# A two-layer hybrid decoder trunk: another emission plan for the small work and the weight splits, and attention scores in two row tiles

## The chip, the cores and the metric

The kernel runs on one core of a Trainium2 chip. The metric is the time of one execution in microseconds (us), as the median of several runs on the device.

## The reference, cut to what matters

The input is 256 tokens of 1024 float32 values, the depth is 2. One layer does:

```python
h = rms_norm(x, attn_norm)
(mq, mk, mv, nq, nkv, ngate, gq, gk, gv, g_lr, g_out, merge) = split(h @ w_in)
o_moba = moba_attention(rms_norm(mq), rms_norm(mk), mv, rel_bias)       # 4 heads of 64
kc, vc = compress_tokens(k_c, ...), compress_tokens(v_c, ...)           # gelu(h @ w1) @ w2
o_nsa  = nsa_attention(rms_norm(nq), kc, vc, k_s, v_s, k_w, v_w, ...)    # 4 heads, 3 branches
o_gla  = gla_attention(gq, gk, gv, log_a)                               # 4 heads, chunks of 64
z = g_a * (o_moba @ w_moba) + g_b * (o_nsa @ w_nsa) + g_c * (o_gla @ w_gla)
x = x + z @ w_out
a, g = split(rms_norm(x) @ w_up)                                        # 2 x 2816 columns
x = x + (gelu(causal_conv3(a)) * g) @ w_down
```

With 256 tokens, MoBA's own block, the selected blocks of NSA and its window all come down to causal softmax attention over the same 256 keys, with a bias by distance. So each layer has 12 softmax heads in three branches: "s" (selected) and "w" (window) of NSA, which share the queries, and "m" (MoBA).

## The kernel before, in words

**Dense products.** Every weight goes through the core once, in blocks of 128x1024 float32 (512 KB). A block is loaded into a `raw` buffer by a DMA of SyncE. ScalarE rounds it to a high part `whi` (type fp32r), and VectorE and GpSimd write what is left, `wlo` = `raw` - `whi`, each for a share of the columns. TensorE then makes three fp32r matmuls per tile into a PSUM buffer `pd`: high by high, low weight by high activation, high weight by low activation. The activations are split in the same way into `hh` and `hl` (in the FFN's down projection `fh` and `fl`). Chunks of mode A have weights as the moving operand (512, 396, 272 or 256 columns); those of mode B have activations (256 columns): the queries and keys of GLA, and all of the FFN's up projection.

**Stages.** Per layer: the input projection (14 chunks), the three branch projections, the output projection, the up projection (22 chunks in pairs j = 0 to 10: `done_a` and `done_g`, lines 1400 and 1434), the down projection. In the up projection each pair has 96 matmuls on TensorE, and beside them VectorE does four `SCALAR_TENSOR_TENSOR` of the convolution, two products with PSUM, one cast (`fh`) and its share of four blocks' low parts; GpSimd does one product (`tt<-tt,rsB`), `fl` and the rest of the low parts.

**What sets the order.** All engines work through their instructions in the order in which the program issues them. This order is made while the program is built: `Plan` (line 51) keeps a clock for each engine (`V` VectorE, `A` ScalarE, `G` GpSimd, `PE` TensorE), `cost` (line 73) estimates an instruction, `note` (line 106) books it and when its output is there. The small work (norms, attention, GLA, evictions) is written as generators, which lie in the lists `urgent` and `normal`. `run_phase` (line 357) issues the dense matmuls and calls `tick` (line 307) after each tile, which lets those generators go on whose time has come by the plan; `avail` and `hold` (lines 200 and 205) make one wait for a planned time, `take` and `give` for a free buffer. A wait in the plan costs nothing on the chip; a wait on the chip arises where an instruction stands in an engine's order ahead of its inputs.

**Weight blocks.** `Pump` (line 218) has 5 `raw` buffers and 3 pairs of `whi`, `wlo`. When `run_phase` gets a block, loads are issued for 5 blocks from there and splits for 2. `split` (line 262) issues the high part on ScalarE and directly behind it the low part, the columns divided so that VectorE and GpSimd end together by their costs, as though neither slowed the other:

```python
v, g = max(plan.t["V"], t0) + 0.07, max(plan.t["G"], t0) + 0.1 + 0.0
m = int((v - g + c * 0.00104) / (0.00104 + 0.0023)) // 64 * 64
```

**Scores.** `softmax_branch` (line 1002) starts two generators with two heads each. `one_head` (line 1053) computes scores with a contraction over all 128 partitions: two heads' queries lie in one tile (64 partitions each), and the key tiles `kt` and `mkt` hold each head with zeros in the other half (`nsa_keys` line 879, `pair_T` with `halves` line 943; the zeros come from memsets on GpSimd at the start). Per head there is one float32 matmul with 128 columns and one with 256; the trace shows each float32 matmul as two records. Then follow the bias and row maximum (VectorE), the exponential (ScalarE), three transposes (TensorE), a copy `pT` (ScalarE) and three matmuls into `po`.

**Compression.** `compress` (line 725) multiplies 16 slices of `w1` with the tokens `xt`, which four additions on VectorE write, in two groups of eight matmuls (`pst<-tt,w`).

Line 135 (line 163 in the changed file) is the helper through which every instruction is recorded, so rows are told apart by their tiles.

Of the kernel before, what the change touches and what calls it, by code (L numbers as in the profile page):

```python
# [18 lines left out]
S = 256  # L19
# [30 lines left out]

class Plan:
# [20 lines left out]

    def cost(self, e, f, outs, ins, kw):
        n = max(_free(a) for a in outs[:1] + ins[:1]) if outs else 0
        if e == "PE":
# [3 lines left out]
            if ins[0].dtype == F32R:  # L79
                return max(0.107, m / 2400 + 0.0025)  # L80
            return max(_free(ins[0]) / 600, m / 600 + 0.004)
        if e == "V":
            if f == "reciprocal":
                return 0.07 + n * 0.0084
            if f == "tensor_tensor_scan":
                return 0.07 + n * 0.00104
# [4 lines left out]
            return 0.07 + 0.06 * ptr + n * (0.00052 if fast else 0.00104)  # L91
        if e == "S":
            return 0.06
        if e == "A":
            if f == "dma_start":
                return 0.06
            return 0.11 + n * 0.00083 + 0.05 * ("pst" in str(ins[0].tensor) or "pd" in str(ins[0].tensor)) + 0.09 * (len(outs) - 1 + hasattr(kw.get("bias"), "tensor"))
# [8 lines left out]
    def note(self, e, f, args, kw):  # L106
        outs, ins = _aps(args, kw)
        if not outs:
            return
        self.n += 1  # L110
        st = max([self.t[e], self.t["PE"]] + [self.get(a) + 0.15 for a in ins])
# [4 lines left out]
        else:  # L116
            en = st + self.cost(e, f, outs, ins, kw)
            self.t[e] = en
        lat = 0.2 if e == "PE" else 0.0
# [33 lines left out]
def trunk_kernel(ctx, tc, x, rel_bias, attn_norm, w_in, moba_q_norm, moba_k_norm,  # L153
# [61 lines left out]
    RAWB, HLB = 5, 3  # L215
    AHEAD_D, AHEAD_S = 5, 2

    class Pump:
        def __init__(self):
# [3 lines left out]
            self.auto = False  # L223

# [37 lines left out]
        def split(self):  # L262
            n, hi, lo = self.open()
            hi(0, n)
            w = self.blocks[self.ns - 1][1]
            h = self.hl[self.ns - 1][0]
            t0 = plan.get(h)
            v, g = max(plan.t["V"], t0) + 0.07, max(plan.t["G"], t0) + 0.1 + 0.0
            c = n * w
            m = int((v - g + c * 0.00104) / (0.00104 + 0.0023)) // 64 * 64  # L270
            m = c if m > c - 128 else m if m >= 128 else 0
# [11 lines left out]
        def get(self):  # L283
            i = self.ng
            self.ng += 1
            self.ahead(AHEAD_D, AHEAD_S if self.auto else 0)
            return self.hl.pop(i)
# [19 lines left out]
    def tick(n=4):  # L307
        now = plan.t["PE"]
        for g in list(urgent):
# [13 lines left out]
    def idle(limit=None):  # L323
# [3 lines left out]
        if a == (len(flags), plan.n) and plan.t["PE"] <= now:  # L327
            r = [ready.get(id(g), 0.0) for g in urgent + normal]
            r = [v for v in r if v > now] + ([limit] if limit else [])
# [285 lines left out]
    def norm_rs(st):  # L615
# [4 lines left out]
        yield  # L620
        V.tensor_scalar(st["rsh"], st["rs"], 0.5, None, op0=OP.mult)
# [19 lines left out]
    def make_layer(l):  # L641
# [41 lines left out]
        def gla_gate():  # L683
# [33 lines left out]
            setf("ln")  # L717
            V.tensor_sub(m, m, u)
# [945 lines left out]
```

## Time and profile before

| what | value |
|---|---|
| median of 3 runs | 852.81 us (852.76 to 854.57) |
| the profiled execution's own time | 854.52 us |
| its span, first to last instruction | 852.7 us |
| TensorE busy | 836.4 us (98%) |
| VectorE / ScalarE / GpSimd busy | 575.4 / 431.7 / 469.4 us |
| granted TensorE clock, mean | 0.995 of full speed |
| DMA, mean over the span | 168 GB/s, 143.57 MB |

The time outside the span is 1.8 us. A busy share is an average over all stages; matmuls overlap in the records, so a busy TensorE is not one at its peak: the number of matmuls that start in a stretch says more than the busy time.

### The profile page before, as it was taken

Reading aid. Unit: us, or ns where it says so; the run is one execution under the profiler, and the core shown is the slowest. Engines: PE = TensorE matmul, PEld = TensorE weight load, DVE = VectorE, ACT = ScalarE, POOL = GpSimd, SP = SyncE. Lnnn points to the kernel's source line nnn. Section 1 sums busy time; section 2 is a strip of 40 time slices with the busy share of each in tenths; the row PEclk is TensorE's granted clock in tenths of the full one; section 3 lists DMA queues with packets and bytes.
Section 4 is the critical chain, followed back from the end, with each engine's and each line's share of the span. In section 5 each row is a group of like instructions: output and inputs, shape, how many; then the busy total and the mean of one; then the engine's idle time right before and its main releaser. Section 6 shows DMA issues by size and latency. Waiting matters only on the chain.

```text
span 852.7 us, 13950 instructions
## 1 busy us (share of the span) xinstructions
PE 836.4 (98%) x5173; PEld 747.5 (88%) x5173; DVE 575.4 (67%) x882; ACT 431.7 (51%) x667; POOL 469.4 (55%) x338
## 2 busy tenths in 40 slices
PE   8999999999999899999999999999999999999998
PEld 7779888888899899998898898888888999999886
DVE  5676887458657878875447667764595599887632
ACT  6545555554456445443557445564544654554431
POOL 5534644546555665666545346535565476665653
PEclk9999999999999999999999999999999999999999
DMA  7893444445555465556458444545556555646561
GB/s 230 255 262 110 124 123 143 118 163 193 178 154 170 149 194 177 174 183 210 158 173 238 136 122 125 148 124 156 166 177 194 162 160 173 196 157 212 184 220 46
DMA packets 109976, 143.57 MB, mean 168 GB/s; under 512 B 13677, under 2 KB 71380, under 8 KB 109780
## 3 DMA queue, kind: packets, MB, share of 16 engines
q1 hardware_dynamic: 109892, 142.68, 53.9%
q8 instruction: 41, 0.67, 0.3%
q14 instruction: 27, 0.22, 0.1%
q10 hardware_dynamic: 16, 0.00, 0.0%
HBM read 141.60 MB, written 2.63 MB: 169 GB/s over the span
## 4 chain that ended last, share of the span: by engine, by line
PE 82%; DVE 7%; issue 1%; POOL 1%; ACT 0%; DVEq 0%; ACTq 0%; POOLq 0%
PE pd L135 72%; PE pst L135 9%; DVE tt L135 4%; DVE wlo L135 3%; PE po L135 2%; POOL tt L135 1%; ACT whi L135 0%; DVE qz L135 0%; POOL fl L135 0%; POOL wlo L135 0%; DVE fh L135 0%; DVE xs L135 0%; DVE grp L135 0%; DVE hl L135 0%; DVEq L135 0%
## 5 line engine op out<-in xcount | busy, mean ns | idle before, releaser
L135 POOL TENSOR_TENSOR wlo<-raw,whi 128x256 fp32r<-128x256 f32 (+10 forms) x219 | 315.1, 1442 | 281.0 <-ACT whi L135 268.6
L135 ACT CAST whi<-raw 128x1024 fp32r<-128x1024 f32 (+3 forms) x268 | 271.7, 1017 | 267.3 <-PE pd L135 156.7
L135 DVE TENSOR_TENSOR wlo<-raw,whi 128x768 fp32r<-128x768 f32 (+8 forms) x262 | 267.2, 1028 | 177.1 <-ACT whi L135 176.3
L135 PE MATMUL pd<-hh,wlo 128*128 128x256 f32 x768 | 218.5, 285 | 4.6 <-DVE wlo L135 4.6
L135 PE MATMUL pd<-hh,whi 128*128 128x256 f32 x768 | 219.8, 286 | 0.2
L135 PE MATMUL pd<-hl,whi 128*128 128x256 f32 x768 | 218.2, 284 | 1.1 <-DVE hl L135 1.1
L135 PE MATMUL pd<-whi,hh 128*128 128x512 f32 (+3 forms) x512 | 204.8, 400 | 1.5 <-ACT whi L135 0.7
L135 PE MATMUL pd<-wlo,hh 128*128 128x512 f32 (+3 forms) x512 | 192.7, 376 | 1.6 <-DVE wlo L135 1.2
L135 PE MATMUL pd<-whi,hl 128*128 128x512 f32 (+3 forms) x512 | 192.2, 375 | 0.0
L135 PEld LDWEIGHTS pd<-hh,wlo 128*128 128x128 f32 x768 | 148.0, 193 | 5.8 <-DVE wlo L135 5.8
L135 PEld LDWEIGHTS pd<-hl,whi 128*128 128x128 f32 x768 | 148.0, 193 | 1.8 <-DVE hl L135 1.5
L135 PEld LDWEIGHTS pd<-hh,whi 128*128 128x128 f32 x768 | 148.0, 193 | 1.3 <-ACT hh L135 0.7
L135 PEld LDWEIGHTS pd<-whi,hh 128*128 128x128 f32 x512 | 96.6, 189 | 17.3 <-ACT whi L135 1.9
L135 PEld LDWEIGHTS pd<-wlo,hh 128*128 128x128 f32 x512 | 96.8, 189 | 16.9 <-DVE wlo L135 2.6
L135 PEld LDWEIGHTS pd<-whi,hl 128*128 128x128 f32 x512 | 96.4, 188 | 17.3
L135 DVE SCALAR_TENSOR_TENSOR tt<-tt,pt 128x255 f32<-128x255 f32 x88 | 84.8, 986 | 1.6
L135 PE MATMUL pd<-whi,fh 128*128 128x512 f32 x176 | 68.7, 391 | 0.0
L135 PE MATMUL pd<-wlo,fh 128*128 128x512 f32 x176 | 68.7, 390 | 0.0
L135 PE MATMUL pd<-whi,fl 128*128 128x512 f32 x176 | 68.5, 389 | 0.0
L135 POOL TENSOR_TENSOR fl<-tt,fh 128x512 fp32r<-128x512 f32 x22 | 40.5, 1840 | 31.6 <-DVE fh L135 31.6
L135 ACT ACTIVATE tt<-tt,nm 128x128 f32<-128x128 f32 (+1 forms) x48 | 21.4, 447 | 41.0 <-DVE nm L135 41.0
L135 ACT ACTIVATE tt<-tt 128x512 f32<-128x512 f32 (+1 forms) x52 | 26.1, 532 | 31.7 <-DVE tt L135 31.6
(211 smaller groups left out, 838.7 us busy)
## 6 DMA issues: line engine op xcount, KB each, us to landing
raw<-in_w_up_dram SPq DMA_DIRECT2D x88, 512.0 KB
raw<-in_w_in_dram SPq DMA_DIRECT2D x84, 512.0 KB
raw<-in_w_down_dram SPq DMA_DIRECT2D x44, 512.0 KB
raw<-in_w_out_dram SPq DMA_DIRECT2D x16, 512.0 KB
raw<-in_w_branch_gla_dram SPq DMA_DIRECT2D x8, 512.0 KB
raw<-in_w_in_dram SPq DMA_DIRECT2D x8, 396.0 KB
raw<-in_w_branch_moba_dram SPq DMA_DIRECT2D x4, 512.0 KB
raw<-in_w_branch_nsa_dram SPq DMA_DIRECT2D x4, 512.0 KB
```

The source lines that it names most:

```text
L135: return g(*args, **kw)
```

## The change

Four things. (1) **The plan's costs** are others: TensorE's matmuls are dearer (a 512-column fp32r tile 0.227 instead of 0.216 us), outputs of VectorE and ScalarE have a delay of their own, inputs count 0.04 us behind their planned end instead of 0.15. The plan also knows intervals (`port`) in which VectorE or GpSimd read two operands from SBUF, and lengthens an instruction of the one by what it overlaps with the other's (`end`). (2) **Low parts** are not issued directly behind the high part but put into a list, from which `poll` takes them when the plan expects the high part within 0.3 us; the shares are found by trying all divisions in steps of 64 with the new lengthening and a charge on GpSimd's columns. There are 4 pairs of `whi`, `wlo`, and splits are issued 3 blocks from the one that is used. (3) **Scores** are computed for two heads together: `kt` and `mkt` hold both heads without zeros, and each matmul contracts over 64 partitions, 0 to 63 for the one head and 64 to 127 for the other, in two PSUM buffers. (4) **Compression** goes in four groups of four matmuls, and some generators wait with `avail` until an input is there by the plan.

```diff
 class Plan:
+        self.port = {"V": [], "G": []}
+        self.kind = (False, 128)
...
+    def ports(self, e, ins):
+        return e in "VG" and sum(_free(a) > 8 for a in ins) > 1 and not any(_psum(a) for a in ins)
+    def end(self, e, st, c):
+        en = st + c
+        for _ in range(4):
+            en = st + c + sum(max(0.0, min(en, b) - max(st, a)) for a, b in self.port["G" if e == "V" else "V"])
+        return en
...
             if ins[0].dtype == F32R:
-                return max(0.107, m / 2400 + 0.0025)
-            return max(_free(ins[0]) / 600, m / 600 + 0.004)
+                return max(0.112, m / 2400 + 0.0135)
+            c = max(0.112 if _free(ins[0]) < 65 else 0.224, m / 600 + 0.008)
+            return c * (0.55 if ins[0].shape[0] == 64 and m > 64 else 1.0)
...
-        st = max([self.t[e], self.t["PE"]] + [self.get(a) + 0.15 for a in ins])
+        st = max([self.t[e], self.t["PE"]] + [self.get(a) + 0.04 for a in ins])
...
+            if e == "PE":
+                k = (ins[0].dtype == F32R, ins[0].shape[0])
+                c += 0.03 * (k[0] != self.kind[0]) + 0.2 * ((k[1] == 64) != (self.kind[1] == 64))
+                self.kind = k
+            en = st + c
+            if self.ports(e, ins):
+                en = self.end(e, st, c)
+                self.port[e] = self.port[e][-30:] + [(st, en)]
             self.t[e] = en
-        lat = 0.2 if e == "PE" else 0.0
+        lat = {"PE": 0.17, "V": 0.09, "A": 0.1}.get(e, 0.03)
...
-    RAWB, HLB = 5, 3
-    AHEAD_D, AHEAD_S = 5, 2
+    RAWB, HLB = 5, 4
+    LEAD = 0.3
+    GX, PORT = 0.0005, 0.0008
+    AHEAD_D, AHEAD_S = 5, 3
...
         def split(self):
             n, hi, lo = self.open()
             hi(0, n)
-            w = self.blocks[self.ns - 1][1]
-            h = self.hl[self.ns - 1][0]
...
+            i = self.ns - 1
+            self.pend.append((i, self.hl[i][0], n, self.blocks[i][1], lo))
+        def poll(self, i=-1):
+            while self.pend and (self.pend[0][0] <= i or plan.get(self.pend[0][1]) <= plan.t["PE"] + LEAD):
+                self.low(*self.pend.pop(0)[1:])
+        def low(self, h, n, w, lo):
             c = n * w
+            best = None
+            for m in [0] + list(range(192, c + 1, 64)):
+                en = []
+                if m < c:
+                    v = max(plan.t["V"], plan.t["PE"], plan.get(h))
+                    en.append(plan.end("V", v, 0.08 + (c - m) * 0.00105))
+                if m:
+                    g = max(plan.t["G"], plan.t["PE"], plan.get(h))
+                    en.append(plan.end("G", g, 0.1 + m * 0.0023 + (GX * (c - m) if m < c else 0.0)))
+                k = max(en) + PORT * m
+                if best is None or k < best[0]:
+                    best = (k, m)
+            m = best[1]
...
     def tick(n=4):
         now = plan.t["PE"]
+        pump.poll()
...
             setf("ln")
+            yield from avail(u)
             V.tensor_sub(m, m, u)
...
-                if a == 0:
-                    yield
+                    if i % 4 == 3 and a + i < 8:
+                        yield from hold(2.0)
...
-            kt = T["kt"] = Z["kt"]
+            kt = atl("kt", [128, 2, S])
             for b in range(2):
-                for hh in range(2):
-                    r = slice(64 * hh, 64 * hh + 64)
-                    V.tensor_scalar(kt[r, b, hh], p[r, b], par[l][0][r, 20 + b:21 + b], None, op0=OP.mult)
+                V.tensor_scalar(kt[:, b], p[:, b], par[l][0][:, 20 + b:21 + b], None, op0=OP.mult)
...
+            for c in range(2):
+                yield from take(sem_t, 2)
+                yield from take(sem_ps, 2)
+                sp = pair_scores(br, c)
+                for i in range(2):
+                    normal.append(rest(2 * c + i, *sp[i]))
+                while left[0] > 2 - 2 * c:
+                    yield
...
+        def pair_scores(br, c):
...
+            sp = [(tt(), pst()) for _ in range(2)]
+            for t in range(2):
+                for i in range(2):
+                    r = slice(64 * i, 64 * i + 64)
+                    o = sp[i][1][:, 0:128] if t == 0 else sp[i][1][:, 128:384]
+                    PE.matmul(o, qT[r, t * 128:t * 128 + 128], kT[r, 0:t * 128 + 128], start=True, stop=True)
+            return sp
```

The rest of a head (`head_rest`) does what `one_head` did behind its scores. The places at which the order counts most:

VectorE at the start of the first layer's up projection, before; `tt<-tt,pt` are the convolution's four instructions of one pair j (two rows of 255 and two of 254 columns), `tt<-pd,rsB`, `tt<-tt,pd` and `fh` the other work of a pair:

```order
L135 TENSOR_TENSOR tt<-pd,rsB 128x512 x2
L135 TENSOR_TENSOR wlo<-raw,whi 128x768 x2
L135 SCALAR_TENSOR_TENSOR tt<-tt,pt 128x255
L135 SCALAR_TENSOR_TENSOR tt<-tt,pt 128x254
L135 SCALAR_TENSOR_TENSOR tt<-tt,pt 128x255
L135 SCALAR_TENSOR_TENSOR tt<-tt,pt 128x254
L135 SCALAR_TENSOR_TENSOR tt<-tt,pt 128x255
L135 SCALAR_TENSOR_TENSOR tt<-tt,pt 128x254
L135 SCALAR_TENSOR_TENSOR tt<-tt,pt 128x255
L135 SCALAR_TENSOR_TENSOR tt<-tt,pt 128x254
L135 TENSOR_TENSOR wlo<-raw,whi 128x768
L135 TENSOR_TENSOR tt<-tt,pd 128x512
```

and now:

```order
L163 TENSOR_TENSOR tt<-pd,rsB 128x512
L163 TENSOR_TENSOR wlo<-raw,whi 128x640
L163 TENSOR_TENSOR wlo<-raw,whi 128x832
L163 SCALAR_TENSOR_TENSOR tt<-tt,pt 128x255
L163 SCALAR_TENSOR_TENSOR tt<-tt,pt 128x254
L163 SCALAR_TENSOR_TENSOR tt<-tt,pt 128x255
L163 SCALAR_TENSOR_TENSOR tt<-tt,pt 128x254
L163 TENSOR_TENSOR tt<-pd,rsB 128x512
L163 TENSOR_TENSOR wlo<-raw,whi 128x640
L163 TENSOR_TENSOR wlo<-raw,whi 128x832
L163 TENSOR_TENSOR tt<-tt,pd 128x512
```

Before, the convolutions of two pairs stand in a row; now each pair's four have low parts on both sides, and the low parts on VectorE are larger.

VectorE in the first layer's input projection, before; `tt<-tt` and `b` belong to GLA's gate and wait for ScalarE's logarithm, `tt<-pst,pt 64x256` are the additions ahead of the compression, `kt` the keys:

```order
L135 TENSOR_TENSOR kn<-a_421,kss 128x2x64 x4
L135 TENSOR_TENSOR wlo<-raw,whi 128x512
L135 TENSOR_SCALAR tt<-pst,pt 128x256 x2
L135 TENSOR_TENSOR tt<-tt 128x512
L135 SCALAR_TENSOR_TENSOR b<-smask,tt 128x512
L135 TENSOR_TENSOR tt<-pst,pt 64x256 x4
L135 TENSOR_TENSOR wlo<-raw,whi 128x384
L135 TENSOR_SCALAR kt<-pst,pt 64x256 x4
```

and now:

```order
L163 TENSOR_TENSOR kn<-a_428,kss 128x2x64 x4
L163 TENSOR_TENSOR wlo<-raw,whi 128x1024
L163 TENSOR_SCALAR tt<-pst,pt 128x256 x2
L163 TENSOR_TENSOR tt<-pst,pt 64x256 x4
L163 TENSOR_TENSOR tt<-pd,nqs 128x256 x2
L163 TENSOR_TENSOR wlo<-raw,whi 128x768
L163 TENSOR_SCALAR kt<-pst,pt 128x256 x2
L163 SCALAR_TENSOR_TENSOR grp<-pd,rsB 128x512
L163 TENSOR_TENSOR tt<-tt 128x512
L163 SCALAR_TENSOR_TENSOR b<-smask,tt 128x512
```

The additions and the keys now stand ahead of the two instructions that wait for the logarithm, and the keys need two instructions instead of four.

TensorE at the first scores of branch "s" in the first layer, before (the last rows of it; the next head's scores follow three dense matmuls and a compression group later):

```order
L135 MATMUL pst<-tt,w_481 128x30 x8
L135 MATMUL pd<-whi,hh 128x512
L135 MATMUL pd<-wlo,hh 128x512
L135 MATMUL pd<-whi,hl 128x512
L135 MATMUL pst<-kt,grp 128x128
L135 MATMUL pst<-kt,grp 128x256
```

and now:

```order
L163 MATMUL pst<-tt,w_445 128x30 x4
L163 MATMUL pst<-kt,grp 128x128 x2
L163 MATMUL pst<-kt,grp 128x256 x2
L163 MATMUL pd<-whi,hh 128x512
L163 MATMUL pd<-wlo,hh 128x512
```

Two heads' scores stand together, and a compression group has four matmuls. Over the whole program VectorE's low parts grow from 262 instructions with 193032 columns to 266 with 213664, and GpSimd's go from 219 with 71608 columns to 221 with 50976; the number and sizes of the dense matmuls are the same.

## Rows read from the trace of the kernel before

**Rows 1.** The page's busy times: engine, busy us (share of the span), instructions.
```profile
PE 836.4 (98%) x5173; PEld 747.5 (88%) x5173; DVE 575.4 (67%) x882; ACT 431.7 (51%) x667; POOL 469.4 (55%) x338
```

**Rows 2.** Busy time by stretch: us, engines' busy us (instructions), granted clock, DMA share, GB/s.
```profile
25.00:60.00 35.00, 32.89 (x176) 26.02 (x175) 24.91 (x53) 17.57 (x28) 16.60 (x15) 0.99 0.89 266
60.00:120.00 60.00, 59.17 (x366) 51.93 (x366) 44.48 (x92) 31.72 (x69) 30.39 (x21) 0.98 0.41 122
...
238.00:245.00 7.00, 6.31 (x46) 5.64 (x45) 3.74 (x7) 4.79 (x10) 2.06 (x2) 1.00 0.61 188
...
262.00:298.00 36.00, 32.87 (x268) 32.07 (x268) 30.32 (x37) 17.16 (x21) 22.81 (x15) 1.00 0.49 149
...
456.00:464.00 8.00, 7.35 (x33) 5.77 (x32) 5.84 (x6) 5.15 (x7) 4.53 (x3) 1.00 0.60 177
...
650.00:690.00 40.00, 39.30 (x300) 37.62 (x299) 26.20 (x37) 23.58 (x37) 22.11 (x15) 1.00 0.56 171
690.00:740.00 50.00, 48.51 (x400) 47.90 (x399) 44.12 (x49) 24.61 (x32) 31.92 (x22) 1.00 0.56 177
...
840.00:853.00 13.00, 8.97 (x40) 7.11 (x38) 2.55 (x4) 1.05 (x1) 2.33 (x2) 0.93 0.11 42
```

**Rows 3.** The chain that ended last, pieces: start us, us, engine and tile.
```profile
179.42 28.61 PE pd L135 x126
...
245.10 8.62 PE pd L135 x72
...
297.00 0.82 DVE wlo L135
```

**Rows 4.** Timeline of DVE and POOL, first GpSimd alone, then both together.
```profile
22.45 0.73 POOL L135 TENSOR_TENSOR wlo<-raw,whi 128x256 fp32r<-128x256 f32 x1 [0.43 <-ACT whi L135]
...
262.95 0.96 DVE L135 TENSOR_TENSOR wlo<-raw,whi 128x768 fp32r<-128x768 f32 x1 [1.96 <-ACT whi L135]
262.99 1.51 POOL L135 TENSOR_TENSOR wlo<-raw,whi 128x256 fp32r<-128x256 f32 x1 [1.40 <-ACT whi L135]
...
263.82 6.72 DVE L135 SCALAR_TENSOR_TENSOR tt<-tt,pt 128x255 f32<-128x255 f32 x8
...
285.94 0.48 DVE L135 TENSOR_TENSOR wlo<-raw,whi 128x320 fp32r<-128x320 f32 x1
```

**Rows 5.** Timeline of PE in the first layer's input projection.
```profile
26.92 0.44 PE L135 MATMUL pst<-ident,ga 128*16 128x128 f32 x2 [0.62 <-ACT ga L135]
...
55.47 0.39 PE L135 MATMUL pd<-whi,hl 128*128 128x512 f32 x1
56.61 1.95 PE L135 MATMUL pst<-tt,w 128*128 128x30 f32 x16 [0.75 <-ACT whi L135]
```

**Rows 6.** Timeline of DVE in the same place.
```profile
53.80 0.69 DVE L135 TENSOR_TENSOR tt<-tt 128x512 f32<-128x512 f32 x1 [2.12 <-ACT tt L135]
...
55.67 1.72 DVE L135 TENSOR_TENSOR tt<-pst,pt 64x256 f32<-64x256 f32 x4
```

**Rows 7.** Timeline of PE: one head's scores between dense matmuls.
```profile
512.59 0.39 PE L135 MATMUL pd<-whi,hl 128*128 128x512 f32 x1
512.81 0.82 PE L135 MATMUL pst<-kt,grp 128*128 128x128 f32 x4
513.28 0.58 PE L135 MATMUL pd<-whi,hh 128*128 128x512 f32 x1
513.70 0.39 PE L135 MATMUL pd<-wlo,hh 128*128 128x512 f32 x1
```

**Rows 8.** Timeline of PE: dense ones round GLA's two gate matmuls (16 rows, 256 columns).
```profile
452.37 0.40 PE L135 MATMUL pd<-whi,hl 128*128 128x512 f32 x1
...
454.08 0.40 PE L135 MATMUL pd<-wlo,hh 128*128 128x512 f32 x1
```

**Rows 9.** Timeline of PE: compression's second product, lower and upper 64 rows.
```profile
482.85 0.39 PE L135 MATMUL pst<-w,gk 64*15 64x128 f32 x2
483.17 0.43 PE L135 MATMUL pst<-w,gv 64*128 64x64 f32 x2
```

More of the change, by code (lines that the diff above doesn't have):

```diff
@@ L48, in _span, with _psum @@
     return lo, lo + 1 + sum(abs(s) * (n - 1) for s, n in ap.ap[1:])
+def _psum(ap):
+    return any(n in str(ap.tensor) for n in ("pst", "pd_", "po_"))
 class Plan:
@@ L85, in cost @@
             if f == "tensor_tensor_scan":
-                return 0.07 + n * 0.00104
+                return 0.09 + n * 0.0021
             if f == "memset":
@@ L107, in note @@
         outs, ins = _aps(args, kw)
+        if f == "preload_act_table_set":
+            self.t[e] = max(self.t[e], self.t["PE"]) + 1.3
         if not outs:
@@ L328, in idle @@
             r = [ready.get(id(g), 0.0) for g in urgent + normal]
+            if pump.pend:
+                r.append(plan.get(pump.pend[0][1]) - LEAD)
             r = [v for v in r if v > now] + ([limit] if limit else [])
@@ L620, in norm_rs @@
         yield
+        yield from avail(st["rs"])
         V.tensor_scalar(st["rsh"], st["rs"], 0.5, None, op0=OP.mult)
@@ L742, in compress @@
             yield
+            yield from avail(kd)
             yield from take(sem_ps)
@@ L896, in nsa_keys @@
             yield from wait(("par", l))
+            yield from avail(sq)
             kn = at.tile([128, 2, 2, 2, 64], F32, name="kn", tag="kdn")
@@ L903, in nsa_keys @@
             yield
+            yield from avail(kn)
             yield from take(sem_ps)
@@ L1010, in softmax_branch, with rest @@
             sums = atl("sm" + br, [128, 2, 2, 4])
-            pend = [1, 1]
-            def heads(i):
-                for h in (i, i + 2):
-                    yield from one_head(br, h, o, sums)
-                pend[i] = 0
-            normal.append(heads(0))
-            yield
-            normal.append(heads(1))
-            while any(pend):
-                yield
+            left = [4]
+            def rest(h, s, p):
+                yield from head_rest(br, h, s, p, o, sums)
+                left[0] -= 1
+            yield from avail(*((T["mqt"], T["mkt"]) if br == "m" else (T["nq"], T["kt"])))
+            for c in range(2):
[6 more added lines that the diff above has]
+                    yield
             sh = [128, 2, 4, 64]
@@ L1059, in one_head @@
                 b = 0 if br == "s" else 1
-                qT, kT = T["nq"][:, h // 2], T["kt"][:, b, h % 2]
                 vv = lambda t: T["vs"][:, t, b]
                 bh = 4 + h
-            yield from avail(qT, kT)
-            yield from take(sem_t)
-            yield from take(sem_ps)
-            s, p = tt(), pst()
-            PE.matmul(p[:, 0:128], qT[:, 0:128], kT[:, 0:128], start=True, stop=True)
-            PE.matmul(p[:, 128:384], qT[:, 128:256], kT, start=True, stop=True)
-            yield
+            yield from avail(p)
             nm = at.tile([128, 2], F32, name="nm", tag="nm", bufs=4)
@@ L1090, in one_head @@
             yield
+            yield from avail(pT)
             PE.matmul(o[:, 0, h], pT[:, 0:128], vv(0), start=True, stop=True)
```

33 lines of the change are left out of this document (14 added, 19 removed).

## The prediction

> **What bounds the kernel now.** I read the busy times first. TensorE is busy for 836.4 of 852.7 us [rows 1], no other engine for more than 67% of the span. So the time is TensorE's own work plus the 16.3 us in which it stands still, and a change pays only if it takes work from TensorE or closes such a gap. VectorE, ScalarE and GpSimd matter only as the ones who are waited for.
>
> Second, the busy times by stretch, to see where the gaps lie. Idle is the width of a stretch less TensorE's busy time: 2.11 us in 25 to 60, 0.83 in 60 to 120, 0.69 in 238 to 245, 3.13 in 262 to 298, 0.65 in 456 to 464, 0.70 in 650 to 690 and 1.49 in 690 to 740 [rows 2]: together 9.6. The other 6.7 us of the 16.3 lie nearly all in the first 25 us and behind 840 us, and nothing in the change touches what is waited for there.
>
> Third, rates, because idle time tells less than is lost: a wait also breaks the overlap of matmuls. In an undisturbed stretch 126 dense matmuls of 512 columns take 28.61 us, 0.227 each, and 72 of 256 columns 8.62 us, 0.120 each [rows 3]. Where the compression starts, the next start comes after 1.14 us instead of 0.227: lost are 0.91 us, of which 0.75 show as idle [rows 5]. In 262 to 298, the start of the first layer's up projection, 268 matmuls ran where 36 / 0.1197 = 301 had room, so 33 x 0.1197 = 3.9 us are lost; in 690 to 740, the same place of the second layer, 50 - 400 x 0.1197 = 2.1 us [rows 2].
>
> Fourth, why there. The chain of waits runs through VectorE's low parts in that stretch, up to the last at 297.00 us [rows 3]. VectorE is busy for 30.3 of 36 us and GpSimd for 22.8 [rows 2], and the timeline shows that they are busy with waiting for each other: 256 columns of a low part take GpSimd 0.73 us alone, but 1.51 us when VectorE began its 768 columns 0.04 us earlier (0.96 us of VectorE, then the remaining 0.55); eight convolution instructions of 255 or 254 columns take 6.72 us, 0.84 each, where a low part of 320 columns takes 0.48 [rows 4]. The Trainium skill (SBUF — State Buffer, section Who interferes with whom) says the same of VectorE with two SBUF inputs against a reading GpSimd, and adds that the loser stands still until the other has finished; the 1.51 us agrees. By that rule a divided low part gains nothing from the division, and the change still divides most of them.
>
> **The change, part by part.**
>
> *Up projection (A).* In the steady part a pair j has four low parts; VectorE's share goes from 1024, 256, 768 and 768 columns to 768, 832, 832 and 1024, so 640 columns move to it from GpSimd. VectorE pays (0.96 - 0.48) / 448 = 1.07 ns per column, 0.69 us; GpSimd is spared 640 x 0.73 / 256 = 1.8 us [rows 4]. Since they exclude each other, the pair of them needs 1.1 us less per 96 matmuls, which take 11.5 us. At the start the backlog also changes: the eight convolutions in a row become twice four with low parts between, low parts no longer hold VectorE while ScalarE's high part is under way (it idled 1.96 us for one at 262.95, GpSimd 1.40 [rows 4]), and splits stand a block further ahead, which is 24 matmuls or 2.9 us. The gap to close is 3.9 + 2.1 = 6.0 us in the two layers; ends are 0 and 6.0. I take 70%, 4.2 us, because the backlog of two pairs at the start remains and only its length shrinks.
>
> *Input projection (B).* The largest gap has a cause that the new order removes: the four additions ahead of the compression ran at 55.67 us, behind two instructions of the gate for which VectorE had stood 2.12 us [rows 6]; they are now ahead of those. The transposes of `ga` (0.62 us idle [rows 5]) come three dense matmuls later. The loads of `w1` pass one weight block in SyncE's queue and are needed in four steps, so they are no new wait; DMA engines are busy 89% there [rows 2], but the bytes are the same. Between 0 and the 2.94 us of both stretches I take 2.0.
>
> *Layer seams (C).* 238 to 245, 456 to 464 and 650 to 690 lose 2.04 us. At the first and third the residual, its norm and the low part of it follow each other, which stays; the second waits for a high part, and one more block of lead covers it. I take 0.6; ends 0 and 2.04.
>
> *Scores in two row tiles (D).* A head's scores cost TensorE from the start at 512.59 to that at 513.70, less two dense matmuls: 1.11 - 0.454 = 0.66 us for 384 columns, or 1.31 for two heads [rows 7]. What it costs to switch to matmuls over fewer rows and back is seen at the gate: 1.71 - 0.454 = 1.26 us for 512 columns, which at full height would take 0.66 x 512 / 384 = 0.88, so 0.38 more [rows 8]. There are 12 pairs of heads. Without overlap a pair costs 1.31 + 0.38, in all 12 x 0.38 = 4.6 us more. With full overlap it costs 0.66 + 0.38 = 1.04, in all 3.3 us less. The nearest row on overlap shows none: the second product of the compression uses rows 0 to 63 and then 64 to 127, and the second pair of records starts 0.32 us behind the first [rows 9]; but their outputs differ in width, so another switch may lie between. Each float32 matmul is two records (x4 for two matmuls [rows 7]), and if records keep their order, the second of one head can run beside the first of the other, which makes 5 steps of 8: in units of 0.11 us for 128 columns and 0.22 for 256, 2 x 0.11 + 3 x 0.22 = 0.88 us. With the switch that is 1.26, and 12 x 0.05 = 0.6 us are gained. I take this middle value, and 4.6 more and 3.3 less as bounds. The Trainium skill (TensorEngine Tiling (Array Packing), section Key Properties) has the rule against this change: another tiling mode drains the engine. The 0.38 us agrees.
>
> *New waits (E).* The plan's allowance for inputs falls from 0.15 to 0.04 us, so some small matmuls will stand where their inputs are just late; `avail` works against it. The other engines' delays that the plan now has partly replace it. Below it is 0, above the 3.9 us of the worst stretch now; since most gaps of before are under 0.9 us and a few will open, I take 1.0.
>
> *Nothing* for the rest: two memsets on GpSimd at the start, three instructions fewer for the keys per layer and the larger `whi`, `wlo` lie beside TensorE, and the low parts that are now issued later have three blocks of lead as cover; if that lead were lost, each block would cost what rows 5 show for one wait, 0.9 us.
>
> Sum: - 4.2 - 2.0 - 0.6 - 0.6 + 1.0 = - 6.4 us. Against the profiled execution's own time of 854.5 that makes 848.1. The median of the runs is 1.7 us below that execution, so I forecast 852.8 - 6.4 = **846.4 us**.
>
> **Rivals.**
>
> *Full overlap of the tiles.* For it speaks that the two heads write to different PSUM buffers and need different rows; against it rows 9. 3.3 instead of 0.6 are gained: 843.7 us. The Trainium skill (TensorE: Matmul & The Clock Gate, Part 3) has the rule for this, that matmuls in different row groups start about 4 ns apart; no run here shows it yet.
>
> *No overlap.* The 0.32 us of rows 9 would be typical. 4.6 lost instead of 0.6 gained: 851.6 us.
>
> *The order returns nothing.* The gaps of A to C shift by a few us and remain; for it speaks that the plan is still a plan, against it that the additions of rows 6 visibly leave a wait. 852.8 - 0.6 + 1.0 = 853.2 us, no change.
>
> *Slower: VectorE becomes the bound in the up projection.* In 262 to 298 it was busy for 30.3 us in 268 / 96 = 2.8 pairs, 10.9 us per pair [rows 2]. With 0.69 us more it stands at 11.6, above the 11.5 of TensorE, if its waits for GpSimd stay as long as they are. From there every 0.1 us costs 22 x 0.1 = 2.2 us; at 11.9 us per pair 8.8 are lost and A is not returned: 852.8 - 2.2 + 8.8 = 859.4 us. It decides from 11.7 on. Against it: GpSimd reads 1.8 us less per pair, which shortens VectorE's waits.
>
> **How the numbers follow.** Forecast 0.55, its own range 842.5 to 849.5, from the ends of A to C, not all at once; full overlap 0.18; no overlap 0.11; nothing returned 0.08; VectorE the bound 0.08. The range of 8 in 10 reaches over full overlap with a good return and over no overlap, up to nothing returned: **841.0 to 853.4 us**. A measurement of this kernel can tell about 0.2%, 1.7 us, from no change. Faster by more are the first two and a part of the third: 0.77; the same 0.14; slower 0.09.
>
> **What would show it.** Right: in the first 36 us of the first up projection 290 or more matmuls start; the convolutions take clearly less than 0.84 us; no wait ahead of the compression; a pair of heads costs 1.2 to 1.3 us between dense matmuls. Wrong: VectorE's low parts still end the waits in the up projection, or a pair costs 1.7 us, or TensorE's small matmuls show new waits of more than 2 us together. The forecast falls if the seams or the first 25 us grow, which I hold as they are.

## The result, and the profile after

Four runs of the changed kernel have a median of **843.85 us** (842.90 to 844.73), four of the kernel before on the same chip 852.78; the ratio is 0.9893, 95% interval 0.9872 to 0.9914. The forecast was 846.4: the sign is right and the time lies in the forecast's own range (842.5 to 849.5), but two terms were too small and three too favourable, so that their errors in part cancelled.

The page's busy times, to be read beside [rows 1]:

```profile
PE 831.8 (99%) x5173; PEld 741.0 (88%) x5173; DVE 571.0 (68%) x880; ACT 430.1 (51%) x667; POOL 418.0 (50%) x338
```

The span is 842.9 us, so TensorE stands still for 11.1 us instead of 16.3. GpSimd has lost 51 us of work, and VectorE has not gained any, though its low parts have 11% more columns. Busy time by stretch, the columns as in [rows 2], first the up projections (the first row is the first 36 us of the first layer's, the second and third lie as far behind their starts as 262 to 298 and 690 to 740 did), then two places in the input projections:

```profile
236.34:272.34 36.00, 35.17 (x290) 34.57 (x288) 24.88 (x36) 22.90 (x36) 15.65 (x14) 1.00 0.49 153
259.07:295.07 36.00, 36.00 (x301) 35.80 (x300) 29.05 (x38) 20.95 (x26) 22.02 (x17) 1.00 0.57 179
682.50:732.50 50.00, 50.00 (x419) 50.00 (x418) 42.05 (x51) 25.58 (x32) 29.10 (x22) 1.00 0.65 194
29.00:34.00 5.00, 4.76 (x15) 3.06 (x16) 4.51 (x9) 3.34 (x10) 3.67 (x5) 0.74 0.58 166
464.00:470.00 6.00, 5.47 (x24) 4.49 (x24) 2.97 (x8) 1.17 (x2) 0.32 (x1) 0.72 0.59 174
```

301 and 419 matmuls where 268 and 400 ran: no wait is left there. The other two rows are new: TensorE had a granted clock of 0.74 and 0.72 (a mix of its levels 2.4 and 1.2 GHz), and ahead of each stand waits. The timeline of TensorE (start, duration, [idle before <- released by]):

```profile
27.37 0.34 PE L163 MATMUL pd<-whi,hl 128*128 128x396 f32 x1
29.01 0.43 PE L163 MATMUL pst<-ident,rs 128*128 128x128 f32 x2 [1.30 <-DMA raw<-in_w_in_dram]
...
461.90 0.55 PE L163 MATMUL pst<-ident,kn 128*128 128x128 f32 x3 [0.42 <-DVE kn L163]
...
463.61 1.08 PE L163 MATMUL pst<-tt,w 128*128 128x30 f32 x8 [0.46 <-DVE tt L163]
465.22 0.80 PE L163 MATMUL pd<-whi,hh 128*128 128x512 f32 x1 [0.53 <-DVE grp L163]
```

and VectorE ahead of the last three:

```profile
459.41 1.23 DVE L163 TENSOR_TENSOR wlo<-raw,whi 128x1024 fp32r<-128x1024 f32 x1 [0.31 <-ACT whi L163]
460.56 1.29 DVE L163 TENSOR_TENSOR kn<-a,kss 128x128 f32<-128x128 f32 x4
461.77 1.01 DVE L163 TENSOR_TENSOR wlo<-raw,whi 128x832 fp32r<-128x832 f32 x1
462.71 1.74 DVE L163 TENSOR_TENSOR tt<-pst,pt 64x256 f32<-64x256 f32 x4
464.48 0.69 DVE L163 SCALAR_TENSOR_TENSOR grp<-pd,rsB 128x512 f32<-128x512 f32 x1
```

`kn` and the four additions ahead of the compression each stand behind a low part of over 1 us, and `grp` stands behind the additions; TensorE's instruction stands ready before they end.

A pair of heads between dense matmuls, to be read beside [rows 7]:

```profile
105.76 0.39 PE L163 MATMUL pd<-whi,hl 128*128 128x512 f32 x1
106.08 0.93 PE L163 MATMUL pst<-kt,grp 64*128 64x128 f32 x8
106.93 0.50 PE L163 MATMUL pd<-whi,hh 128*128 128x512 f32 x1
107.27 0.39 PE L163 MATMUL pd<-wlo,hh 128*128 128x512 f32 x1
```

Eight records for two heads take 0.93 us where four for one head took 0.82. From 105.76 to 107.27 less two dense matmuls the pair costs 1.51 - 0.454 = 1.06 us, before 1.31.

**Where the time went.** For each phase I add up, over TensorE's records, the distance from one start to the next less that of the same kind in undisturbed stretches (scores counted at full height in both). "Of it the clock" is, over stretches of 10 us, their width times what the granted clock lacks of 1; outside the input projections and the last few us only the first up projection of the kernel before has such a dip of the clock, of 1.7 us. All this is one execution, the profiled one, whose own time stands beside the median; in some rows it is the slowest or the fastest. "Span x clock" is the span of every execution with a clock on record times that mean granted clock, lowest to highest: an estimate of the span without dips, good to 0.4 us.

| kernel | median us | profiled us | span x clock | input 1 | up 1 | input 2 | up 2 | of inputs 1 / 2 the clock |
|---|---|---|---|---|---|---|---|---|
| before | 852.78 | 854.52 | 848.2 to 850.9 | 13.6 | 6.8 | 3.6 | 3.4 | 1.7 / 0 |
| after | 843.85 | 844.73 | 839.0 to 839.5 | 10.7 | 1.6 | 4.5 | 1.3 | 1.7 / 1.7 |
| row tiles alone | 857.04 | 856.38 | 848.4 to 849.3 | 17.6 | 5.1 | 3.2 | 3.5 | 5.2 / 0 |
| after, heads in turn | 843.89 | 843.13 | 839.4 to 841.2 | 10.0 | 1.6 | 3.4 | 1.3 | 1.7 / 0 |
| after, low parts at once | 860.77 | 861.23 | 848.3 to 849.2 | 21.5 | 2.2 | 9.6 | 1.3 | 6.8 / 3.4 |
| after, lead of two | 844.68 | 845.25 | 840.6 to 841.8 | 11.1 | 2.8 | 2.1 | 2.6 | 1.7 / 0 |
| after, old division | 859.21 | 858.30 | 850.1 to 851.6 | 17.7 | 1.4 | 11.2 | 1.2 | 3.4 / 1.7 |
| after, low parts on VectorE | 840.89 | 841.42 | 837.1 to 839.1 | 8.6 | 1.8 | 2.8 | 1.6 | 1.8 / 0 |
| after, old costs | 847.21 | 847.21 | 840.9 to 842.4 | 14.4 | 2.5 | 1.8 | 1.7 | 3.4 / 0 |
| before, new costs | 861.00 | 860.97 | 855.8 to 856.8 | 17.3 | 3.7 | 7.7 | 4.1 | 3.5 / 0 |
| before, new dense cost | 873.52 | 871.49 | 867.7 to 868.9 | 11.5 | 9.2 | 12.8 | 7.9 | 0 / 1.7 |
| after, on VectorE, lead of two | 846.59 | 850.35 | 842.2 to 843.2 | 16.4 | 2.7 | 1.8 | 2.4 | 5.1 / 0 |
| row tiles and lead of three | 860.70 | 862.67 | 848.2 to 852.3 | 22.5 | 2.3 | 8.6 | 1.2 | 3.4 / 5.1 |
| row tiles and late low parts | 857.38 | 863.70 | 849.2 to 851.8 | 15.9 | 2.8 | 15.2 | 3.2 | 5.1 / 6.9 |

### The profile page after: what moved, and what is told of

It reads as the page before. It is cut to its first block, busy times and chain, and to the rows that moved or that the text cites. A ratio compares the mean times of both kernels' runs of the same rounds, so it can differ in the third digit from the quotient of the medians.

```text
span 842.9 us, 13919 instructions
## 1 busy us (share of the span) xinstructions
PE 831.8 (99%) x5173; PEld 741.0 (88%) x5173; DVE 571.0 (68%) x880; ACT 430.1 (51%) x667; POOL 418.0 (50%) x338
## 4 chain that ended last, share of the span: by engine, by line
PE 91%; DVE 3%; issue 2%; POOL 2%; ACT 1%; DMA 0%; SPq 0%; POOLq 0%; DVEq 0%; ACTq 0%
PE pd L163 80%; PE pst L163 9%; PE po L163 2%; POOL wlo L163 2%; DVE wlo L163 1%; ACT whi L163 1%; DVE tt L163 1%; DVE xs L163 0%; POOL tt L163 0%; DVE hl L163 0%; ACT hh L163 0%; DVE boot L163 0%; DVE m L163 0%; DMA tt<-in_moba_k_norm_dram 0%; DVE kn L163 0%
## 5 line engine op out<-in xcount | busy, mean ns | idle before, releaser
L163 POOL TENSOR_TENSOR wlo<-raw,whi 128x192 fp32r<-128x192 f32 (+7 forms) x221 | 264.3, 1199 | 302.9 <-ACT whi L163 264.5
L163 DVE TENSOR_TENSOR wlo<-raw,whi 128x832 fp32r<-128x832 f32 (+8 forms) x266 | 286.3, 1087 | 136.6 <-ACT whi L163 136.0
L163 PEld LDWEIGHTS pd<-wlo,hh 128*128 128x128 f32 x512 | 98.1, 192 | 16.3 <-DVE wlo L163 1.5
L163 DVE SCALAR_TENSOR_TENSOR tt<-tt,pt 128x255 f32<-128x255 f32 x88 | 69.6, 811 | 1.6
L163 POOL TENSOR_TENSOR fl<-tt,fh 128x512 fp32r<-128x512 f32 x22 | 45.7, 2079 | 30.7 <-DVE fh L163 28.1
L163 PEld LDWEIGHTS pd<-whi,fl 128*128 128x128 f32 x176 | 33.0, 188 | 6.9
```

Source lines behind the costliest of these rows:

```text
L163: return g(*args, **kw)
```

## The experiments

Each ratio is to the kernel before on the same chip, whose median lay between 853.7 and 854.4 us beside these runs.

**1. Row tiles alone** (before, with the changes to `kt`, `mkt`, `pair_T` and the scores).

> The kernel before with nothing but the scores in two row tiles (and the dense key tiles that they need); plan, division of the low parts and lead as before. Theory of overlap: two heads' records run beside each other, a pair costs 1.06 us of TensorE where two heads cost 1.31, 12 pairs gain about 3 us: 849.5 to 850.5 us. Rival, no overlap, only the switch of rows: a pair costs 1.7 us and the time is 856 to 858 us. Rival, the gain of the whole change lies in the order alone: within 1 us of 852.8.

Measured 1.0034 (1.0020 to 1.0049): the time lies in the range of the second expectation, but not for its reason. The overlap was there, a pair costs 1.06 us here too (read at 118.6). The old plan, which does not know the new instructions, adds a wait of 0.34 us ahead of the first scores (59.95) and one of 1.67 us (132.60), and behind the first the granted clock is 0.64, 0.50 and 0.58 over three times 4 us from 60 on. Without the dips this kernel is level with the one before (span x clock). No run takes the tiles out of the change, so what they are worth there is read from the cost of a pair alone.

**2. Heads in turn**, so that neighbouring records use the same rows:

```diff
-            for t in range(2):
-                for i in range(2):
+            for i in range(2):
+                for t in range(2):
```

> The changed kernel with the two loops of the score matmuls exchanged: both matmuls of the one head, then both of the other. Theory that records start in the order in which they are issued, so that only neighbours in different rows overlap: a pair costs about 1.3 + 0.38 - 0.11 = 1.6 us instead of 1.06, 12 pairs lose 6 us: about 850 us. Rival, tiles overlap whatever the order: 844 us as the changed kernel.

Measured 0.9882 (0.9865 to 0.9898), and the pair costs the same:

```profile
105.25 0.39 PE L163 MATMUL pd<-whi,hl 128*128 128x512 f32 x1
105.56 0.93 PE L163 MATMUL pst<-kt,grp 64*128 64x128 f32 x8
106.43 0.50 PE L163 MATMUL pd<-whi,hh 128*128 128x512 f32 x1
106.76 0.39 PE L163 MATMUL pd<-wlo,hh 128*128 128x512 f32 x1
```

1.51 us again. In the trace each record of the one head has its counterpart of the other 13 ns behind it (in the changed kernel 7 ns), though now all of the first head's are issued first: the tiles run as two streams whatever the order of issue. The Trainium skill (TensorE: Matmul & The Clock Gate, Part 3) gives about 4 ns between starts in different row groups and says that matmuls keep program order; the first is near, the second does not hold in these records.

**3. Low parts at once**, directly behind the high part:

```diff
-            self.pend.append((i, self.hl[i][0], n, self.blocks[i][1], lo))
+            self.low(self.hl[i][0], n, self.blocks[i][1], lo)
```

> The changed kernel with each low part issued directly behind its high part again. If VectorE's and GpSimd's waits for high parts at the head of their queues made the gaps: 2 to 5 us slower, 846 to 849 us, with VectorE's idle time for high parts back above 170 us. If the gaps came from the load that the two put on each other or from the lead: within 1 us of 844.

Measured 1.0077 (1.0060 to 1.0095), slower than either expectation. The up projections stayed closed; the input projections lost 16 us more. VectorE's waits, summed (engine, line waited for: us, times, longest), after and then in this kernel:

```profile
DVE wlo L163 <- ACT whi L163: 136.0, 114, 3.6
```

```profile
DVE wlo L163 <- ACT whi L163: 191.5, 147, 4.4
```

and what that does, on VectorE, ScalarE and TensorE:

```profile
56.45 1.03 DVE L163 TENSOR_TENSOR wlo<-raw,whi 128x832 fp32r<-128x832 f32 x1 [3.05 <-DMA w<-in_cmp_k_w_dram]
57.39 2.08 DVE L163 COPY kd<-a 128x256 f32<-128x256 f32 x2
```

```profile
52.90 1.28 ACT L163 ACT_TABLE_LOAD   x1
54.19 1.29 ACT L163 ACTIVATE tt<-tt 128x512 f32<-128x512 f32 x2
55.39 1.98 ACT L163 CAST whi<-raw 128x1024 fp32r<-128x1024 f32 x2
```

```profile
58.13 0.47 PE L163 MATMUL pst<-ident,kd 128*128 128x128 f32 x1 [3.73 <-DVE kd L163]
```

A low part at the head of VectorE's queue waits for its high part, which ScalarE only begins at 55.39, behind the gate's table load and logarithm (the DMA that the view names is not what it waits for); small work behind the low part (`kd`) makes TensorE wait. So with a lead of three late issue pays in the input projections, not in the up projection.

**4. Lead of two blocks** (`RAWB, HLB = 5, 3`, `AHEAD_D, AHEAD_S = 5, 2`).

> The changed kernel with 3 pairs of high and low buffers and splits 2 blocks ahead, as before the change. If the lead closed the gaps of the up projections: 4 to 7 us slower, 848 to 851 us. If the joint load of VectorE and GpSimd did: within 1.5 us of 844, and the new wait of TensorE at 27 us, where VectorE stands behind a block whose load has not landed, should shrink from 1.3 us to under 0.7.

Measured 0.9886 (0.9867 to 0.9906): level with the change. The third block is worth 2.5 us in the up projections (2.8 + 2.6 against 1.6 + 1.3), and the second input projection is 2.4 us better without it, 1.7 of them the clock. The wait of TensorE at 27 us fell only from 1.30 to 1.02 us, not to under 0.7 as expected.

**5. Old division** (`ports` returns False; the old formula for `m`).

> The changed kernel with a plan that knows nothing of VectorE and GpSimd lengthening each other, and with the old rule for dividing a low part. Theory that their exclusion made the gaps: the up projections lose 4 to 8 us again, 848 to 852 us. Rival, the lead or the deferral did it: within 1 us of 844.

Measured 1.0063 (1.0043 to 1.0083), neither expectation. The up projections stayed closed, the input projections lost 13.7 us more, in waits for `kn`, `tt` and `qz` behind VectorE.

**6. All low parts on VectorE:**

```diff
-            for m in [0] + list(range(192, c + 1, 64)):
+            for m in [0]:
```

> The changed kernel with all low parts on VectorE and none on GpSimd (but the two tiles at the start). If the two exclude each other, a division gains nothing: per pair of the up projection VectorE has 4 x 1.22 + 4 x 0.48 + 1.8 = 8.6 us of 11.5, and the up projections lose no more than now; the input projections, where VectorE has more other work, may lose 1 to 3 us: 843 to 847 us. Rival, VectorE becomes the bound without GpSimd's help: the up projections lose 5 us and more, above 849 us.

Measured **0.9841** (0.9809 to 0.9873), the best of all: 840.89 us (839.17 to 842.54), no run of it as slow as the fastest of the change, and faster than both expectations. The groups of VectorE and GpSimd (count | busy, mean ns of one | idle before), after:

```profile
L163 DVE TENSOR_TENSOR wlo<-raw,whi 128x832 fp32r<-128x832 f32 x163 | 188.8, 1161 | 125.0 <-ACT whi L163 124.7
L163 DVE SCALAR_TENSOR_TENSOR tt<-tt,pt 128x255 f32<-128x255 f32 x44 | 40.9, 929 | 0.0
...
L163 DVE SCALAR_TENSOR_TENSOR tt<-tt,pt 128x254 f32<-128x254 f32 x44 | 30.5, 692 | 1.6
...
L163 POOL TENSOR_TENSOR wlo<-raw,whi 128x192 fp32r<-128x192 f32 x163 | 201.9, 1241 | 222.5 <-ACT whi L163 197.4 <-DVE grp L163 13.9 <-DVE xs L163 4.4
```

and here:

```profile
L163 DVE TENSOR_TENSOR wlo<-raw,whi 128x1024 fp32r<-128x1024 f32 x248 | 318.6, 1292 | 153.3 <-ACT whi L163 152.6
L163 DVE SCALAR_TENSOR_TENSOR tt<-tt,pt 128x255 f32<-128x255 f32 x44 | 24.7, 560 | 0.0
L163 DVE SCALAR_TENSOR_TENSOR tt<-tt,pt 128x254 f32<-128x254 f32 x44 | 23.1, 525 | 1.6
```

A block divided 832 to 192 takes VectorE 1.16 us and GpSimd 1.24; undivided it takes VectorE 1.29. 1.24 us of GpSimd buy 0.13 us, and the convolutions pay for it: 0.93 and 0.69 us against 0.56 and 0.53. VectorE's total rises only from 571.0 to 578.7 us, GpSimd's falls from 418 to 151. This is the rule of the Trainium skill (SBUF — State Buffer, section Who interferes with whom) that I set beside [rows 4], that the loser of the shared port stands still. The trace agrees in the main: 192 columns take GpSimd 0.59 us in the changed kernel where it began first (28.89), and 1.24 on average beside 832 of VectorE.

TensorE does not gain where the convolutions are: the up projections lose 0.5 us more than in the change. The gain lies in the input projections (10.7 to 8.6 and 4.5 to 2.8), and 1.7 us of it is a dip of the clock in the second that this execution lacks. By span x clock the gain is 1.2 us on average (839.25 to 838.05), so more than half of the 3.0 us between the medians is fewer dips. The order is another one here too, since the plan books the undivided low parts differently; that was not told apart from the division.

**7. Old costs.** The change with the old figures for TensorE, VectorE and ScalarE, their delays and the margin of 0.15 us.

> The change with all the old costs, delays and the old margin of the plan (0.216 us for a dense matmul, delays 0.2 and 0, margin 0.15); late low parts, their new division, the lead of three and the row tiles stay. Theory: what closed the gaps of the up projection is the costs, since late issue, division and lead each failed to bring them back: TensorE loses 4 to 6 us in the first up projection and 3 in the second again (now 1.6 and 1.3), and the time is 849 to 852 us. Rival: several parts close the same gaps, each by itself; then the up projections lose under 2 us each here too, and the time stays within 843 to 847 us.

Measured 0.9915 (0.9887 to 0.9944), nearest to the rival, though the first up projection loses 2.5 us instead of under 2. The costs are worth 1.3 us in the up projections, and what else they bring lies in the first input projection (14.4 against 10.7); the second is 2.7 us better without them, 1.7 of it the clock.

**8. New costs alone**, in the kernel before.

> The kernel before with all the new costs, delays and margin of the plan and nothing else of the change. Theory (the costs close the up projection): the up projections lose under 2.5 us each (before 6.8 and 3.4), which is 6 to 8 us; the input projections may lose more or less; 846 to 850 us. Rival (several parts are needed together, or the structure does it): the first up projection still loses over 5 us, and the time is within 2 us of before.

Measured 1.0086 (1.0067 to 1.0105). The first up projection fell to 3.7 us, the second rose to 4.1: neither theory. The input projections lost 7.8 us more.

**9. The new dense cost alone**, in the kernel before:

```diff
-                return max(0.107, m / 2400 + 0.0025)
+                return max(0.112, m / 2400 + 0.0135)
```

> The kernel before with the new cost of TensorE's dense matmuls alone (0.227 instead of 0.216 us for 512 columns, 0.120 instead of 0.109 for 256). Theory (a plan whose TensorE is 10% too quick in the up projection issues VectorE's work too late against it): the up projections lose 3 us or less each, time 847 to 851 us. Rival (the delays and margin matter, or the structure): both lose as before, 6.8 and 3.4 us, time 852 to 856 us.

Measured 1.0228 (1.0202 to 1.0254), and theory and rival both fall: the true cost of a matmul, put alone into the old plan, gives the slowest kernel of all. Two pairs late in the second up projection, on VectorE:

```profile
751.74 0.69 DVE L135 TENSOR_TENSOR tt<-tt,pd 128x512 f32<-128x512 f32 x1 [1.88 <-POOL tt L135]
...
753.40 3.41 DVE L135 TENSOR_TENSOR wlo<-raw,whi 128x1024 fp32r<-128x1024 f32 x2
...
761.52 0.96 DVE L135 TENSOR_TENSOR wlo<-raw,whi 128x768 fp32r<-128x768 f32 x1 [1.16 <-ACT whi L135]
764.36 0.69 DVE L135 TENSOR_TENSOR tt<-tt,pd 128x512 f32<-128x512 f32 x1 [1.88 <-POOL tt L135]
```

They repeat every 12.62 us, where 96 matmuls take 11.5. VectorE stands 1.88 us for GpSimd's product, which has its own low part ahead of it, and 1.16 us for a high part; GpSimd stands 3.46 us for that same high part (761.56), and ScalarE, which makes it, 4.36 us for VectorE's convolution (759.91). None of the three is full; they wait for each other, and a round takes longer than TensorE's 11.5 us. This is the slower rival of the prediction, VectorE lengthened by its waits until it is the bound, in another plan and with ScalarE in it. TensorE loses 1.1 us per pair by it, 0.85 of it idle.

**10. All on VectorE, lead of two** (experiments 4 and 6 together).

> The change with all low parts on VectorE and the lead of two blocks (three pairs of buffers). All low parts on VectorE took 3.0 us off the change, the lead of two 2.5 us off the second input projection and put 2.5 us on the up projections. If the gaps of the second input projection that both closed are the same ones, 841 to 843.5 us, no better than VectorE alone; if the two add, 839 to 840.5 us.

Measured 0.9924 (0.9895 to 0.9952); both expectations missed. The second input projection did fall to 1.8 us, but the first rose to 16.4, with a clock of 0.67 from 30 to 40 us and two new waits for low parts, 1.79 us at 100.88 and 1.42 at 126.18. The profiled run is the slowest; the other three (846.0 to 847.1 us) have a clock of 0.998 instead of 0.994, so part of the 16.4 is not in them. The gains of these two orders do not add.

**11. Row tiles and a lead of three**, nothing else (experiment 1 with `HLB` 4, `AHEAD_S` 3).

> The kernel with the row tiles alone (857.0 us; its up projections lose 5.1 and 3.5 us) and four pairs of buffers with splits three blocks ahead, nothing else of the change. In the runs so far every kernel with a lead of three lost at most 2.5 us in an up projection and every kernel with a lead of two lost 2.4 to 9.2. Theory (the lead is what is common to them): 2.5 us or less each, some 4 to 5 us together. Rival (the lead only helps with late issue or the new division beside it): over 4 and over 3 us. The input projections keep or raise their waits, so the time is 850 to 854 us by the theory, 856 to 860 by the rival.

Measured 1.0081 (1.0052 to 1.0110). The theory holds in the up projections: 5.1 and 3.5 us become 2.3 and 1.2, which is 5.0 of the 5.6 us that the change closes there. The input projections lose 10.3 us more, so the kernel is slower than forecast by either. In the change the same third block costs them 2.0 us (15.2 against 13.2 with a lead of two): what else the change does there makes the lead affordable; which part of it, no run tells.

**12. Row tiles and late low parts** (experiment 1 with the list and `poll`; old division, old costs, lead of two).

> The kernel with the row tiles alone (857.0 us) and low parts issued late, by the list and the plan's time; old division, old costs, lead of two. Theory (late issue is what the input projections gain by, as undoing it cost 10.9 and 5.1 us there): the input projections lose 4 us or more less than the 17.6 and 3.2 us of the row tiles alone, time 850 to 854 us; the up projections keep 3 us or more each, since the lead is still two. Rival (late issue needs the third block of lead as cover): new waits for low parts in the up projections, 5 us or more each, time 856 to 862 us.

Measured 1.0033 (1.0003 to 1.0062), runs from 851.7 to 863.7; the profiled run is the slowest, so its row holds more clock than most have. Up projections 2.8 and 3.2, nearly as the theory said, but only the first input projection improved. In the second, one wait of 1.93 us ahead of 489.16 is followed by this (stretches as above):

```profile
486.00:490.00 4.00, 2.07 (x12) 1.53 (x10) 3.34 (x5) 0.69 (x1) 2.33 (x3) 0.99 0.00 0
490.00:504.00 14.00, 14.00 (x68) 13.22 (x68) 7.47 (x24) 5.22 (x13) 3.11 (x2) 0.52 0.36 114
504.00:510.00 6.00, 6.00 (x55) 6.00 (x54) 4.56 (x6) 3.40 (x5) 3.54 (x2) 1.00 0.29 88
```

14 us at 0.52: 14 x 0.48 = 6.7 us behind a wait of 1.9. The spans of the ten executions go from 849.9 to 861.9 us at clocks from 1.000 down to 0.986; times their clocks they are 849.2 to 851.8. So the clock makes nearly all of the spread.

## Why the prediction was right, and where it was not

The sum was - 6.4 us; the medians differ by 8.9, the spans of the two profiled executions by 9.8. By terms, from the table and so for the 9.8:

- **A, up projection: forecast 4.2, ends 0 and 6.0; measured 7.6**, which is above the end: 6.8 + 3.4 - 1.6 - 1.3 = 7.35, and the seams' waits, which grew by 0.27, are in it. Two steps failed. "I take 70%" assumed that a backlog remains; none does. And the gap to close was not 6.0. I ended the stretch at 298, where the wait ended, but its price went on:

```profile
290.00:294.00 4.00, 4.00 (x35) 4.00 (x35) 2.04 (x5) 1.46 (x2) 2.67 (x3) 1.00 0.77 234
298.00:302.00 4.00, 4.00 (x22) 4.00 (x23) 2.83 (x4) 1.84 (x3) 2.69 (x2) 0.57 0.76 233
302.00:306.00 4.00, 4.00 (x36) 4.00 (x35) 3.32 (x5) 1.96 (x2) 1.29 (x1) 1.00 0.48 164
```

  In the kernel before, TensorE has a clock of 0.57 behind the 2.49 us of standing still and is called fully busy: 4 x 0.43 = 1.7 us. 6.0 + 1.7 = 7.7 is what was there to close in this execution. Not in each: 16 of 39 other executions of that kernel have a mean clock of 0.999, which leaves no room for a dip of 1.7 us. The prediction had no term for the clock at all. As to the cause, I spoke of the division, the convolutions between low parts, late issue and the lead as one; the runs tell them apart. The lead alone closes 5.0 us (11), late issue alone 2.6 (12); taken away singly, only the lead leaves more than 1.3 us open. The division costs nothing there when undone. They overlap, so no share of the 7.6 belongs to one part, and the convolutions between low parts were not tried alone.
- **B, input projection: 2.0; measured 1.4** (13.6 - 10.7 = 2.9, of which D makes 1.5). The wait ahead of the first compression is gone, as forecast, and 60 to 120 us has no idle time. But a wait came behind 27.37, which loses 1.5 us by the starts (the one ahead of the same `rs` was 0.31 us before): the norm's `ms`, from which GpSimd makes `rs`, stands behind two low parts on VectorE, the second of a block just loaded. The view names that block's DMA; `rs` is ready at 28.96.

```profile
26.04 1.81 DVE L163 TENSOR_TENSOR wlo<-raw,whi 128x704 fp32r<-128x704 f32 x2
27.78 0.15 DVE L163 TENSOR_TENSOR ms<-ss 128x2 f32<-128x2 f32 x1
28.21 0.75 POOL L163 TENSOR_TENSOR rs<-ms,mhalf 128x2 f32<-128x2 f32 x1 [2.17 <-DVE ms L163]
```

  I had held the first 25 us as they were, and that holds by TensorE's idle time, 2.77 us after 3.02.
- **C, seams: 0.6; measured 0.3 more** at the first and third: the wait for the residual's low part is 0.97 instead of 0.83 us and 0.96 instead of 0.84. The second seam did lose its wait (0.65 us of idle time in 456 to 464), as forecast; it lies in the second input projection, so that gain is counted in E.
- **D, scores: 0.6 by partial overlap; measured 3.1**, 12 x (1.31 - 1.06), from the pairs that stand between dense matmuls of 512 columns. The step "if records keep their order ... 5 steps of 8" failed: the records of the two heads do not wait for each other. Full overlap, to which I gave 0.18, forecast 1.04 us per pair and 3.3 us; the 0.38 us for the switch, taken from [rows 8], fits with it. [Rows 9] misled; why the second pair of records starts 0.32 us late there was not tried.
- **E, new waits: 1.0; measured 2.5** in the second input projection (4.5 - 3.6, plus the 1.5 that D gains there). Its idle time is only 0.42 + 0.46 + 0.53 = 1.41 us, the clock behind it 6 x 0.28 = 1.7; less the 0.65 us of the second seam that makes 2.5. Without such a dip the same waits cost less: in experiment 2 they are there too, at a clock of 1.00, and that phase loses 3.4.
- The down projections lose 0.5 us less; no term had them. - 7.6 - 1.4 + 0.3 - 3.1 + 2.5 - 0.5 = - 9.8.

A, D and the down projections gave 6.4 us more than forecast, B, C and E 3.0 less. That these offset each other is luck; without it the time would have been below its own range.

Of the signs named beforehand, 290 matmuls started in the first 36 us of the first up projection, just the bound. But this sign could tell nothing: the kernel before starts 291 there, because its waits come later.

```profile
239.27:275.27 36.00, 35.31 (x291) 34.71 (x290) 24.98 (x35) 23.02 (x36) 18.98 (x14) 1.00 0.52 160
```

The convolutions are not clearly below 0.84 us: their mean is (929 + 692) / 2 = 0.81, and before it was (903 + 1069) / 2 = 0.99 over the whole program:

```profile
L135 DVE SCALAR_TENSOR_TENSOR tt<-tt,pt 128x254 f32<-128x254 f32 x44 | 47.0, 1069 | 1.6
L135 DVE SCALAR_TENSOR_TENSOR tt<-tt,pt 128x255 f32<-128x255 f32 x44 | 39.7, 903 | 0.0
```

"A pair costs 1.2 to 1.3" and "no wait ahead of the compression" (it moved to the second layer) were wrong. Of the signs against the forecast one came, two seams grew by 0.27 us together, and one nearly: the waits of small matmuls for `rs`, `kn` and `tt` are 1.30 + 0.42 + 0.46 = 2.18 us, of which 0.31 stood there before, and the bound was 2.

What stays open: why late issue and the new division gain in the input projections only together (undone singly 21.5 and 17.7 us instead of 10.7 in the first, late issue alone 15.9). The waits differ from plan to plan, and no run shows a single cause. No run takes the row tiles, or the new compression with its `avail`, out of the change.

## What to carry to other kernels

In this kernel a part of a tuned order could not be valued by itself: of the nine runs that put one part into the old order or took one out of the new (all but 2, 6 and 10), six ended slower than their starting point and three (4, 7, 12) level with it, though the whole is 8.9 us faster. Price a wait of TensorE with what the clock does behind it, and read the granted clock of the stretch that follows, since a TensorE at half clock counts as busy. Before dividing work between VectorE and GpSimd, compare what the division takes from the one with what it costs the other and everything that shares their port.

## What was not expected of the hardware

- Two row tiles of 64 rows run side by side in float32, with starts 7 or 13 ns apart, in either order of issue; changing to them and back costs about 0.4 us per pair, if the overlap is full (1.06 - 0.66).
- Behind a wait of TensorE of 2.49 us the clock took another 1.7 us (0.57 over 298 to 302 before), behind one of 1.93 us 6.7 us (0.52 over 490 to 504, experiment 12); waits of 1.67 us (132.60, experiment 1) and of 0.85 us, one per pair (experiment 9), were followed by no dip. The profiled runs of the change and of experiment 2 have the same three waits at the second compression, and the clock fell behind them in the first alone. The clock also spreads the runs of one kernel: of 12.0 us between the spans in experiment 12, 2.6 are left when each is taken times its clock.
- GpSimd's share of 192 columns takes 1.24 us beside VectorE's 832, though 256 alone took 0.73 [rows 4].
